# A hybrid mLSTM layer: half of four projections' lo tiles by an adding transfer, and gate_a's modulation on the vector engine

## The chip, the core and the metric

The kernel runs on one core of a Trainium2 chip. A core has five engines that each work through a queue of their own in order: TensorE (PE; its weight loads are listed apart as PEld), VectorE (DVE), ScalarE (ACT), GpSimd (POOL) and SyncE (SP). They meet through semaphores. Transfers between the chip's memory (HBM) and the core's memory (SBUF) run on 16 DMA engines and are issued by SP, ACT or POOL. The metric is the device time of one execution in microseconds. Before the change it is 1696.96 us, the median of three runs (1695.77 to 1698.8).

## What is computed

One layer of a flow-matching backbone on 128 context tokens and 256 latent tokens, model width 2048, all in 32-bit floats.

```python
mod = silu(cond) @ ada_w + ada_b            # six vectors of 2048: shift_a, scale_a, gate_a, shift_f, scale_f, gate_f
h = rmsnorm(x, norm_w[0]) * (1 + scale_a) + shift_a
q, k, v, o, g, u = split(h @ w_in)          # q, k, v, o: 1024 columns each
hm = mlstm_bidir(q, k, v, gates(g))         # 8 heads x 128, chunks of 128 tokens, both directions
hm = rmsnorm(hm) * sigmoid(o)
hp = pool_mixer(u)
mix = concat(hm, hp) @ w_out
x = x + gate_a * rmsnorm(mix, norm_w[1])
h = rmsnorm(x, norm_w[2]) * (1 + scale_f) + shift_f
x = x + gate_f * rmsnorm(square(relu(h @ w1)) @ w2, norm_w[3])
```

The context tokens are modulated by `c_ctx`, the latent tokens by `c`, so each of the six vectors exists twice. Outputs are both token groups and the context's final mLSTM states.

## The kernel before

**Splitting.** TensorE multiplies 32-bit data in a fast format that keeps part of the mantissa (`F32R`). To stay exact, each operand is split into hi, its rounding to that format, and lo = raw - hi, and each product is three matmuls, hi*hi, hi*lo and lo*hi (`mm3`, L142 to L145). A weight tile is 128 x 1024. `load_w` (L122) issues its load on SP (L128, tile `raw`, 3 buffers), makes hi by a copy on ScalarE (L134, 4 buffers) and lo by a subtraction on VectorE (L135, 4 buffers). A raw buffer is free again when lo is done.

**Projections.** `gemm_T` (L168) computes 256 columns of a projection for all 384 tokens. The 2048 rows of the weight come as four tiles (`korder`), so a group of 256 columns has four steps of 24 matmuls. After each step it calls feeds: generators that put one more piece of other work into the program. A `Feed` (L150) has a rate, the mean number of pieces in a step.

**Stages.** First come u, v and the gates' columns (L400 on), then q and k for head pair 0 with the pooling and the gates beside, then q and k for head pairs 1 to 3 with the attention of the pair before beside (L735), then o in four groups (L757), then the output projection `wo` in eight groups, two of them together at the start (L805). Behind it follow the norm, `make_h2` (L915) and the MLP. POOL issues the loads and stores of the attention's states (L579, L685), computes the pow of the norms (L200), and reloads the transposed input for `make_h2` (xTr, L899, 16 transfers of 192 KB).

**Modulation.** A modulation vector is a matrix-vector product with columns of `ada_w`, 8 MB for 1024 columns. It is done in two ways. `ada_mat` (L215) multiplies loaded pieces with the condition on TensorE (L232) and folds the result with L241. `ada_vec` (L261) takes 1024 columns; for each of 16 loads of 512 KB (L269) VectorE multiplies and adds for both conditions (L280, L282), then TensorE sums over partitions (L293), ScalarE copies (L295) and TensorE transposes (L299). Before the change, feed `ada1` runs `ada_mat` for the second half of gate_a (vector 2) at 0.35 pieces a step from q of pair 0 on. Feed `ada2` runs `ada_vec` five times, over scale_f, shift_f and the first half of gate_a, at 1.5 pieces a step in q and k, 1.3 in o, 1.3 in wo. Both must be done when wo ends (L813).

**Order.** Behind the opening projections no order is written out by hand. A scheduler of the recording layer places the instructions of each engine from the program, its dependencies and the buffers.

Of the kernel before, what the change touches and what calls it, by code (L numbers as in the profile page):

```python
# [7 lines left out]
F32 = mybir.dt.float32  # L8
F32R = mybir.dt.float32r
AF = mybir.ActivationFunctionType  # L10
ALU = mybir.AluOpType
# [24 lines left out]
RATE_GS = 0.25  # L36
S_FIRST, S_LAST, N_LAST = 1, 6, 2
LAG = 4
RATES = (1.5, 1.3, 1.3)
RATE_MAT = 0.35  # L40


# [1 line left out]
def hymba_kernel(  # L44
# [6 lines left out]
    nc = tc.nc  # L51
# [13 lines left out]
    def bank(name):  # L65
        return psum.tile([P, 512], F32, tag="ps", name=name)
# [52 lines left out]
    abias = prmT[:, 80:176].rearrange("p (i k) -> p i k", k=KT)  # L119


    def load_w(pieces, name, n=1024, after=(), later=None):  # L122

        raw = wp.tile([P, 1024], F32, tag="raw", name=f"raw_{name}", bufs=3)
        a = pieces[0][1].shape[1]
        rv = raw[:, 0:n].rearrange("p (a b) -> p a b", a=a)
        for off, src in pieces:
            load_w.ins = nc.sync.dma_start(rv[:, :, off:off + src.shape[2]], src).ins  # L128
        hi = wp.tile([P, 1024], F32R, tag="hi", name=f"hi_{name}", bufs=N_W)
        lo = wp.tile([P, 1024], F32R, tag="lo", name=f"lo_{name}", bufs=N_W)  # L130
        with ExitStack() as es:
            for ins in after:
                es.enter_context(tc.issue_after(ins))
            nc.scalar.activation(hi[:, 0:n], raw[:, 0:n], AF.Copy)  # L134
            low = lambda: nc.vector.tensor_tensor(lo[:, 0:n], raw[:, 0:n], hi[:, 0:n].bitcast(F32), op=ALU.subtract)  # L135
            if later is None:
                low()
            else:
                later.append(low)
        return (hi[:, 0:n].rearrange("p (a b) -> p a b", a=a), lo[:, 0:n].rearrange("p (a b) -> p a b", a=a))  # L140

    def mm3(ps, lh, ll, rh, rl, start, stop):  # L142
        nc.tensor.matmul(ps, lh, rh, start=start, stop=False)  # L143
        nc.tensor.matmul(ps, lh, rl, start=False, stop=False)  # L144
        mm3.ins = nc.tensor.matmul(ps, ll, rh, start=False, stop=stop).ins  # L145

    def wview(w):
        return w.rearrange("(k p) n -> p k n", p=P)
# [19 lines left out]
    def gemm_T(w, cols, xs, n, evac, feeds=(), korder=(0, 1, 2, 3), name="g", hold=None):  # L168

        wv = wview(w)  # L170
        acc = {}
        for g, c0 in enumerate(cols):
            for o in range(2):
                acc[g, o] = bank(f"acc_{name}_{c0}_{o}")
        beside = hold or (lambda ki, g: steps_done[-LAG] if len(steps_done) >= LAG else ())
        for ki, kc in enumerate(korder):
            for g, c0 in enumerate(cols):
                hi, lo = load_w([(0, wv[:, 4 * kc:4 * kc + 4, c0:c0 + 256])], f"{name}_{c0}_{kc}", after=beside(ki, g))
                for k in range(4):
                    xh, xl = xs(4 * kc + k)  # L180
                    for o in range(2):
                        mm3(acc[g, o][:, 0:n], hi[:, k, o * P:(o + 1) * P], lo[:, k, o * P:(o + 1) * P],
                            xh[:, 0:n], xl[:, 0:n], ki == 0 and k == 0, ki == 3 and k == 3)
                steps_done.append([])
                for f in feeds:
                    f()
        for g, c0 in enumerate(cols):
            for o in range(2):
                evac(c0 // P + o, acc[g, o])

# [24 lines left out]
    def ada_mat(parts, tags=("ada",), raws=None):  # L215


        n, nk = len(parts), parts[0][2]
        w, nj = nk * P, 8 // nk
        ps = bank(f"ada_{parts[0][0]}_{parts[0][1]}")  # L220
        for b, (i, k0, _) in enumerate(parts):
            c0 = i * D + k0 * P
            for j0 in range(0, 16, nj):
                tag = tags[b % len(tags)]
                raw = raws.pop(0) if raws else None
                if raw is None:
                    raw = (wp if tag == "lo" else adap).tile([P, nj, w], F32, tag=tag, name=f"ada_raw_{i}_{k0}_{j0}", bufs=N_W if tag == "lo" else N_ADA)
                    nc.sync.dma_start(raw, aw[:, j0:j0 + nj, c0:c0 + w])
                for a in range(nj):
                    j = j0 + a  # L230
                    g = j % 4
                    nc.tensor.matmul(ps[32 * g:32 * g + 32, 0:w], cT[:, j, 6 - 2 * b:38 - 2 * b], raw[:, a, :],  # L232
                                     start=b == 0 and j < 4, stop=b == n - 1 and j >= 12)
                if b < n - 1 or j0 + nj < 16:
                    yield
        sb = adap.tile([P, 512], F32, tag="adasb", name=f"ada_sb_{parts[0][0]}_{parts[0][1]}", bufs=1)
        with tc.high_priority():
            nc.scalar.activation(sb[:, 0:w], ps[:, 0:w], AF.Copy)
        yield
        for k in range(nk):  # L240
            nc.tensor.matmul(ps[:, 256 + 8 * k:256 + 8 * k + 2 * n], sb[:, k * P:(k + 1) * P], cst[:, C_SEL, 0:2 * n], start=True, stop=True)  # L241
# [19 lines left out]
    def ada_vec(i, c, n):  # L261


        acc = vec["acc"].tile([P, 2, n], F32, tag="adaacc", name=f"ada_acc_{i}_{c}", bufs=1)
        c0, nj = i * D + c, vec["slab"] // n

        def load(t):
            raw = vec["pool"].tile([P, nj, n], F32, tag="ada", name=f"ada_raw_{i}_{c}_{t}", bufs=vec["bufs"])
            nc.sync.dma_start(raw, aw[:, nj * t:nj * t + nj, c0:c0 + n])  # L269
            return raw  # L270

        raw = load(0)
        yield
        for t in range(16 // nj):
            ahead = load(t + 1) if t < 16 // nj - 1 else None
            for a in range(nj):
                for g in range(2):
                    cj = sg[:, g, nj * t + a:nj * t + a + 1]
                    if t == 0 and a == 0:
                        nc.vector.tensor_scalar(acc[:, g, :], raw[:, a, :], cj, None, op0=ALU.mult)  # L280
                    else:
                        nc.vector.scalar_tensor_tensor(acc[:, g, :], raw[:, a, :], cj, acc[:, g, :], op0=ALU.mult, op1=ALU.add)  # L282
            raw = ahead
            if ahead is not None:
                yield
        yield
        w = n // 2
        nk = w // P
        ps = bank(f"adav_{i}_{c}")
        for h in range(2):  # L290
            for g in range(2):
                r = 32 * (2 * h + g)
                nc.tensor.matmul(ps[r:r + 32, 0:w], ones[:, 0:32], acc[:, g, h * w:(h + 1) * w], start=True, stop=True)  # L293
        sb = vec["pool"].tile([P, 512], F32, tag="adasb", name=f"adav_sb_{i}_{c}", bufs=1)
        nc.scalar.activation(sb[:, 0:w], ps[:, 0:w], AF.Copy)  # L295
        yield
        pf = bank(f"adaf_{i}_{c}")
        for k in range(nk):
            nc.tensor.matmul(pf[:, 4 * k:4 + 4 * k], sb[:, k * P:(k + 1) * P], ident[:, 0:P:32], start=True, stop=True)  # L299
# [100 lines left out]
    for s in range(NS):  # L400
        for ci, (kind, c0, w) in enumerate(chunks):
            k0, nk = ksteps[s]
            hi, lo, n = w_first if s == 0 and ci < 2 else load_chunk(s, ci, h_ins if s == 0 else ())
# [299 lines left out]
        yield  # L703

    def mid_vec():
        for i, q in ((4, 0), (4, 1), (3, 0), (3, 1), (2, 0)):
            yield from ada_vec(i, 1024 * q, 1024)

    ada1 = Feed(ada_mat([(2, 8 + 2 * b, 2) for b in range(4)]), RATE_MAT)
    ada2 = Feed(mid_vec(), RATES[0])  # L710

    def qk(g, feeds):
# [26 lines left out]

    ada2.rate = RATES[1]  # L740
    mixs = [None] * KT
# [296 lines left out]
    pieces = [(a, min(a + NTOK, D)) for a in range(0, D, NTOK)]  # L1038
# [264 lines left out]
```

## Time and profile before

| | |
|---|---|
| median of the runs shown | 1696.96 us |
| profiled execution | 1692.67 us, span 1690.6 us |
| granted TensorE clock, mean | 0.998 |
| HBM read, written | 308.61 MB, 10.51 MB |
| chain that ended last | PE 88%, DVE 6%, DMA 3%, issue 2%, ACT 1% |
| raw_wo: from issue to landing | 4.0 / 5.0 / 7.5 us (least, median, longest) |

Times in views of the profile are microseconds from the start of the span, durations of groups nanoseconds. A row of a stretch gives, for each engine, the busy time and the instructions, then the granted clock, the mean busy share of the 16 DMA engines and what they moved. A row of waits reads: engine, its line and tile, what it waited for; us in total, times, longest. In a row of the timeline stand start, length, engine, line, operation, tiles, and in brackets the idle time before it with what ended it. A row of a tile has the least, median and longest duration in ns. SPq is SP's issuing of transfers.

The chain that ended last lies on TensorE for 88% of the span, so the first question to any change is what it takes from or adds to TensorE's stream, and the second what TensorE would have to wait for.

### The profile page before, as it was taken

Reading aid. Unit: us, or ns where it says so; the run is one execution under the profiler, and the core shown is the slowest. Engines: PE = TensorE matmul, PEld = TensorE weight load, DVE = VectorE, ACT = ScalarE, POOL = GpSimd, SP = SyncE. Lnnn points to the kernel's source line nnn. Section 1 sums busy time; section 2 is a strip of 40 time slices with the busy share of each in tenths; the row PEclk is TensorE's granted clock in tenths of the full one; section 3 lists DMA queues with packets and bytes.
Section 4 is the critical chain, followed back from the end, with each engine's and each line's share of the span. In section 5 each row is a group of like instructions: output and inputs, shape, how many; then the busy total and the mean of one; then the engine's idle time right before and its main releaser. Section 6 shows DMA issues by size and latency. Waiting matters only on the chain.

```text
span 1690.6 us, 28001 instructions
## 1 busy us (share of the span) xinstructions
PE 1663.2 (98%) x11025; PEld 1582.6 (94%) x11025; DVE 1340.0 (79%) x2013; ACT 751.7 (44%) x1225; POOL 133.2 (8%) x181
## 2 busy tenths in 40 slices
PE   6999999999999999999999999999999999999997
PEld 3878899999999989988999999999999999999996
DVE  3677759898989959997798589888588488588688
ACT  4432345555534345543444444444444444444443
POOL 0000002221000024530000000000000000000120
PEclk9999999999999999999999999999999999999999
DMA  9889958777788863754556245444344443433653
GB/s 304 292 287 300 298 164 259 234 250 246 239 285 285 277 224 122 220 155 132 159 173 193 89 137 179 153 150 140 110 150 124 127 137 113 149 122 111 186 184 134
DMA packets 262291, 320.95 MB, mean 190 GB/s; under 512 B 14752, under 2 KB 231440, under 8 KB 261776
## 3 DMA queue, kind: packets, MB, share of 16 engines
q1 hardware_dynamic: 254352, 303.41, 56.3%
q0 software_dynamic: 5856, 13.69, 2.8%
q10 hardware_dynamic: 1952, 2.07, 0.4%
q8 instruction: 86, 1.41, 0.3%
q14 instruction: 45, 0.37, 0.1%
HBM read 308.61 MB, written 10.51 MB: 189 GB/s over the span
## 4 chain that ended last, share of the span: by engine, by line
PE 88%; DVE 6%; DMA 3%; issue 2%; ACT 1%; POOL 0%; DVEq 0%; SPq 0%; ACTq 0%; POOLq 0%
PE acc_w L144 10%; PE acc_w L143 10%; PE acc_w L145 10%; PE y L1137 4%; PE y L1138 4%; PE y L1136 4%; PE u L414 3%; PE v L414 3%; PE acc_wo L143 2%; PE acc_wo L144 2%; PE acc_wo L145 2%; PE ada L232 2%; PE y_yz L1136 2%; PE y_yz L1137 2%; PE y_yz L1138 2%; PE y L980 2%
## 5 line engine op out<-in xcount | busy, mean ns | idle before, releaser
L144 PE MATMUL acc_w<-h2l,hi_w 128*128 128x384 f32 (+1 forms) x1024 | 345.9, 338 | 0.5 <-DVE h2l L930 0.5
L143 PE MATMUL acc_w<-h2h,hi_w 128*128 128x384 f32 (+1 forms) x1024 | 344.4, 338 | 1.2 <-ACT h2h L926 1.2
L145 PE MATMUL acc_w<-h2h,lo_w 128*128 128x384 f32 (+1 forms) x1024 | 345.6, 337 | 0.0
L135 DVE TENSOR_TENSOR lo_w<-raw_w,hi_w 128x1024 fp32r<-128x1024 f32 x152 | 185.4, 1221 | 134.8 <-ACT hi_w L134 134.4
L134 ACT ACTIVATE hi_w<-raw_w 128x1024 fp32r<-128x1024 f32 x152 | 160.7, 1058 | 213.2 <-PE acc_w L144 99.5
L282 DVE SCALAR_TENSOR_TENSOR ada_acc<-ada_raw,sg,ada_acc 128x1024 f32<-128x1024 f32 (+1 forms) x240 | 253.1, 1085 | 2.7 <-DMA ada_raw<-in_ada_w_dram 2.7
L143 PEld LDWEIGHTS acc_w<-h2h,hi_w 128*128 128x128 f32 x1024 | 192.2, 188 | 2.9 <-ACT h2h L926 2.0
L144 PEld LDWEIGHTS acc_w<-h2l,hi_w 128*128 128x128 f32 x1024 | 192.4, 188 | 1.2 <-DVE h2l L930 0.8
L145 PEld LDWEIGHTS acc_w<-h2h,lo_w 128*128 128x128 f32 x1024 | 192.4, 188 | 0.3 <-DVE lo_w L135 0.2
L1122 ACT ACTIVATE hi_t<-w 128x1024 fp32r<-128x1024 f32 x104 | 109.5, 1059 | 116.7 <-DVE w L1158 31.8
L1123 DVE TENSOR_TENSOR lo_t<-w,hi_t 128x1024 fp32r<-128x1024 f32 x104 | 126.3, 1220 | 15.2 <-ACT hi_t L1122 14.9
L1123 DVE TENSOR_TENSOR lo_b<-w,hi_b 128x1024 fp32r<-128x1024 f32 x78 | 95.3, 1221 | 42.2 <-ACT hi_b L1122 41.9
L1122 ACT ACTIVATE hi_b<-w 128x1024 fp32r<-128x1024 f32 x78 | 82.6, 1059 | 101.2 <-PE acc_w L144 67.9
L134 ACT ACTIVATE hi_wo<-raw_wo 128x1024 fp32r<-128x1024 f32 x32 | 34.0, 1064 | 74.9 <-DMA raw_wo<-in_w_out_dram 42.8
L856 ACT ACTIVATE z<-acc_w 128x384 f32<-128x384 f32 x54 | 26.2, 485 | 75.3 <-PE acc_w L145 75.3
L414 PE MATMUL v<-hi_v,hh 128*128 128x384 f32 (+1 forms) x144 | 47.8, 332 | 0.0
L414 PE MATMUL v<-lo_v,hh 128*128 128x384 f32 (+1 forms) x144 | 46.5, 323 | 0.0
L414 PE MATMUL v<-hi_v,hl 128*128 128x384 f32 (+1 forms) x144 | 46.5, 323 | 0.0
L232 PE MATMUL ada<-ada_raw,cT 128*32 128x256 f32 x656 | 45.0, 394 | 1.2 <-DMA ada_raw<-in_ada_w_dram 1.1
L135 DVE TENSOR_TENSOR lo_wo<-raw_wo,hi_wo 128x1024 fp32r<-128x1024 f32 x32 | 38.9, 1221 | 7.3 <-ACT hi_wo L134 7.2
L143 PE MATMUL acc_k<-hh,hi_k 128*128 128x384 f32 x128 | 44.5, 348 | 0.0
L143 PE MATMUL acc_o<-hh,hi_o 128*128 128x384 f32 x128 | 44.1, 344 | 0.0
(2250 smaller groups left out, 4517.1 us busy)
## 6 DMA issues: line engine op xcount, KB each, us to landing
ada_raw<-in_ada_w_dram SPq DMA_DIRECT2D x170, 512.0 KB, 4.8
raw_w<-in_w_dram SPq DMA_DIRECT2D x152, 512.0 KB, 4.2
w<-in_w_dram SPq DMA_DIRECT2D x104, 512.0 KB, 4.2
raw_wo<-in_w_out_dram SPq DMA_DIRECT2D x32, 512.0 KB, 5.0
raw_u<-in_w_in_dram SPq DMA_DIRECT2D x16, 512.0 KB, 8.6
raw_q<-in_w_in_dram SPq DMA_DIRECT2D x16, 512.0 KB, 5.0
raw_k<-in_w_in_dram SPq DMA_DIRECT2D x16, 512.0 KB, 5.0
raw_o<-in_w_in_dram SPq DMA_DIRECT2D x16, 512.0 KB, 4.9
```

Of the source, the lines that this page charges most:

```text
L134: nc.scalar.activation(hi[:, 0:n], raw[:, 0:n], AF.Copy)
L135: low = lambda: nc.vector.tensor_tensor(lo[:, 0:n], raw[:, 0:n], hi[:, 0:n].bitcast(F32), op=ALU.subtract)
L143: nc.tensor.matmul(ps, lh, rh, start=start, stop=False)
L144: nc.tensor.matmul(ps, lh, rl, start=False, stop=False)
L145: mm3.ins = nc.tensor.matmul(ps, ll, rh, start=False, stop=stop).ins
L282: nc.vector.scalar_tensor_tensor(acc[:, g, :], raw[:, a, :], cj, acc[:, g, :], op0=ALU.mult, op1=ALU.add)
L414: nc.tensor.matmul(acc[i][:, 0:n], h[k0 + k][a][:, i * P:(i + 1) * P], (hi, lo)[b][:, k, :], start=k == 0 and a + b == 0, stop=k == nk - 1 ...
L1122: nc.scalar.activation(hi, raw, AF.Copy)
L1123: nc.vector.tensor_tensor(lo, raw, hi.bitcast(F32), op=ALU.subtract)
L1136: nc.tensor.matmul(acc, xh, wh, start=start and j == 0, stop=False)
L1137: nc.tensor.matmul(acc, xh, wl, start=False, stop=False)
L1138: nc.tensor.matmul(acc, xl, wh, start=False, stop=stop and j == 3)
```

## The change

In the second and fourth step of each group of q, k, o and wo, `load_w` is called with `by_dma`. ScalarE then writes -hi into the lo tile, and POOL issues a transfer that adds raw to it in place. That is 40 of the 80 tiles. The second half of gate_a moves from `ada_mat` to a sixth `ada_vec`, with the rates raised so that six fit, and `ada_vec` has one more `yield`, between ScalarE's copy and the transposing matmuls, so that a step of other work lies between them.

```diff
-RATES = (1.5, 1.3, 1.3)
+LO_BY_DMA = ('q', 'k', 'o', 'wo')
+RATES = (1.85, 1.7, 1.55)
@@ load_w
+            if by_dma:
+
+                nc.scalar.activation(lo[:, 0:n], hi[:, 0:n].bitcast(F32), AF.Copy, scale=-1.0)
+                nc.gpsimd.dma_start(lo[:, 0:n].bitcast(F32), raw[:, 0:n], accum_op=ALU.add)
+            elif later is None:
-            if later is None:
                 low()
@@ gemm_T
+                by_dma = name in LO_BY_DMA and ki % 2 == 1
+                hi, lo = load_w([(0, wv[:, 4 * kc:4 * kc + 4, c0:c0 + 256])], f"{name}_{c0}_{kc}", after=beside(ki, g), by_dma=by_dma)
@@ ada_vec
         nc.scalar.activation(sb[:, 0:w], ps[:, 0:w], AF.Copy)
+        yield
         yield
@@ hymba_kernel
-        for i, q in ((4, 0), (4, 1), (3, 0), (3, 1), (2, 0)):
-            yield from ada_vec(i, 1024 * q, 1024)
-
-    ada1 = Feed(ada_mat([(2, 8 + 2 * b, 2) for b in range(4)]), RATE_MAT)
+        for i in (4, 3, 2):
+            for q in range(2):
+                yield from ada_vec(i, 1024 * q, 1024)
+
+    ada1 = Feed(iter(()), RATE_MAT)
```

Lines behind the first hunk are one higher in the changed kernel, behind `load_w` five, behind `gemm_T`'s hunk six, behind the yield seven and behind `mid_vec` eight.

The rows below are the built programs' orders. In tile names the buffer's number stands last; the number before it in a weight tile is the tile's place among the four of its group (wo takes them in the order 2, 3, 0, 1, so 3 and 1 are the adding ones).

ScalarE in wo, before, one group's copies to hi and, between them, the squares and copies of the group before:

```order
L134 ACTIVATE hi_wo_1_5698<-raw_wo_1_5696 128x1024
L134 ACTIVATE hi_wo_2_5745<-raw_wo_2_5743 128x1024
L295 ACTIVATE adav_sb_1024_5657<-adav_1024_5652 128x512
L134 ACTIVATE hi_wo_3_5779<-raw_wo_3_5777 128x1024
L134 ACTIVATE hi_wo_0_5817<-raw_wo_0_5815 128x1024
```

and in the changed program:

```order
L135 ACTIVATE hi_wo_1_5675<-raw_wo_1_5673 128x1024
L139 ACTIVATE lo_wo_1_5676<-hi_wo_1_5675 128x1024
L135 ACTIVATE hi_wo_2_5728<-raw_wo_2_5726 128x1024
L135 ACTIVATE hi_wo_3_5760<-raw_wo_3_5758 128x1024
L139 ACTIVATE lo_wo_3_5761<-hi_wo_3_5760 128x1024
L135 ACTIVATE hi_wo_0_5798<-raw_wo_0_5796 128x1024
```

Each adding tile has a second copy, -hi into lo, directly behind its first.

POOL at the end of wo, before: nothing of wo's weights, and the reloads of xT follow the store of the final normaliser:

```order
L685 DMA out_dram<-C_3_0_1_4413 128x2x128
L200 TENSOR_TENSOR rsh<-rsh,mhalf 128x2 x3
L765 DMA out_dram<-n_o 16x128
L899 DMA xTr_6348<-xT_dram 128x384
L899 DMA xTr_6350<-xT_dram 128x384
```

and in the changed program, where the reloads come behind the last adding transfer:

```order
L140 DMA lo_wo_1_6159<-raw_wo_1_6156 128x1024
L140 DMA lo_wo_3_6244<-raw_wo_3_6241 128x1024
L140 DMA lo_wo_1_6314<-raw_wo_1_6311 128x1024
L907 DMA xTr_6360<-xT_dram 128x384
L907 DMA xTr_6362<-xT_dram 128x384
```

Sixteen adding transfers of wo stand in POOL's queue, and the xTr loads now follow all of them.

SP in wo, before, loads of the weight (`raw_wo`) and of `ada_w` for the vector matvec (`ada_raw`, last but one number: the load's place among 16):

```order
L128 DMA raw_wo_2_5897<-in_w_out_dram 128x4x256
L269 DMA ada_raw_0_6_5927<-in_ada_w_dram 128x1024
L128 DMA raw_wo_3_5935<-in_w_out_dram 128x4x256
L269 DMA ada_raw_0_7_5931<-in_ada_w_dram 128x1024
L128 DMA raw_wo_0_5969<-in_w_out_dram 128x4x256
L269 DMA ada_raw_0_8_5965<-in_ada_w_dram 128x1024
L128 DMA raw_wo_1_6003<-in_w_out_dram 128x4x256
```

and in the changed program:

```order
L129 DMA raw_wo_1_5998<-in_w_out_dram 128x4x256
L275 DMA ada_raw_1024_4_5956<-in_ada_w_dram 128x1024
L275 DMA ada_raw_1024_5_5990<-in_ada_w_dram 128x1024
L129 DMA raw_wo_2_6045<-in_w_out_dram 128x4x256
L275 DMA ada_raw_1024_6_5994<-in_ada_w_dram 128x1024
L275 DMA ada_raw_1024_7_6029<-in_ada_w_dram 128x1024
L129 DMA raw_wo_3_6083<-in_w_out_dram 128x4x256
```

Between the first load of wo's weight and the first of w1's, SP has 40 loads for the vector matvec now where it had 34, beside the same 32 of the weight and 8 for gate_f. In q and k of pairs 1 to 3 there are 32 loads of `ada_w` where there were 35, and in o 21 where there were 24.

More of the change, by code (lines that the diff above doesn't have):

```diff
@@ L119, in hymba_kernel, with load_w @@
     abias = prmT[:, 80:176].rearrange("p (i k) -> p i k", k=KT)
-    def load_w(pieces, name, n=1024, after=(), later=None):
+    def load_w(pieces, name, n=1024, after=(), later=None, by_dma=False):
         raw = wp.tile([P, 1024], F32, tag="raw", name=f"raw_{name}", bufs=3)
@@ L177, in gemm_T @@
             for g, c0 in enumerate(cols):
-                hi, lo = load_w([(0, wv[:, 4 * kc:4 * kc + 4, c0:c0 + 256])], f"{name}_{c0}_{kc}", after=beside(ki, g))
+                by_dma = name in LO_BY_DMA and ki % 2 == 1
+                hi, lo = load_w([(0, wv[:, 4 * kc:4 * kc + 4, c0:c0 + 256])], f"{name}_{c0}_{kc}", after=beside(ki, g), by_dma=by_dma)
                 for k in range(4):
```

## The prediction

> **What bounds the kernel now.** I read the page's busy shares first, then stretches of the run with the DMA share beside the engines, then who waits for whom in the stage that is fullest.
>
> ```profile
> PE 1663.2 (98%) x11025; PEld 1582.6 (94%) x11025; DVE 1340.0 (79%) x2013; ACT 751.7 (44%) x1225; POOL 133.2 (8%) x181
> ```
>
> TensorE is busy 98% of the span, so a change can only win by taking work off it, and can lose wherever it makes it wait. The stretches below are the opening projections (0 to 190), two short samples, q and k of head pairs 1 to 3 (257 to 394), o (394 to 478) and the output projection wo (478 to 618).
>
> ```profile
> core 0: us, PE busy (x) PEld busy (x) DVE busy (x) ACT busy (x) POOL busy (x), PEclk, DMA share, GB/s
> 0.00:190.00 190.00, 174.18 (x1248) 136.52 (x1249) 118.81 (x260) 69.13 (x117) 4.73 (x15) 0.99 0.90 298
> 10.00:15.00 5.00, 0.95 (x2) 0.36 (x2) 0.00 (x0) 3.93 (x9) 0.00 (x0) 1.00 1.02 395
> 257.00:394.00 137.00, 137.00 (x904) 130.17 (x903) 125.77 (x215) 72.11 (x204) 29.95 (x26) 1.00 0.76 245
> 394.00:478.00 84.00, 84.00 (x534) 79.28 (x538) 73.44 (x110) 40.74 (x95) 9.23 (x8) 1.00 0.75 247
> 478.00:618.00 140.00, 140.00 (x819) 137.05 (x812) 124.54 (x141) 50.31 (x76) 9.49 (x17) 1.00 0.88 289
> 500.00:510.00 10.00, 10.00 (x59) 10.00 (x58) 10.00 (x9) 3.09 (x3) 0.00 (x0) 1.00 1.00 343
> ```
>
> In all stages that change, TensorE has no idle time. Second come two things at once in wo: VectorE with 124.54 of 140 us, and the 16 DMA engines with a share of 0.88. In 500 to 510 they stand at 1.00 and move 343 GB/s; the fastest stretch of the trace moves 395. In the opening, where transfers set the pace, the share is 0.90 over 190 us, so 0.88 is already near what a long stage reaches.
>
> ```profile
> SPq L269 <- DVE ada_acc L282: 56.3, 27, 3.6
> SPq L128 <- DVE lo_wo L135: 27.3, 28, 2.4
> PEld acc_wo L143 <- ACT hi_w L134: 0.8, 1, 0.8
> ```
>
> These are waits in wo. Loads wait for VectorE to free their buffers (56.3 + 27.3 us), while TensorE's own waits are tenths of a us: the buffers' depth hides VectorE. So work taken from VectorE buys nothing by itself here.
>
> **The change, part by part.** *gate_a's second half leaves TensorE.* The matrix form ran 16 steps (four column pieces by four loads) of eight L232 matmuls, spread over q, k and o, and one L241 step.
>
> ```profile
> 295.34 0.34 PE L145 MATMUL acc_k<-hh,lo_k 128*128 128x384 f32 x1
> 295.61 0.64 PE L232 MATMUL ada<-ada_raw,cT 128*32 128x256 f32 x8
> 296.18 0.44 PE L143 MATMUL acc_k<-hh,hi_k 128*128 128x384 f32 x1
> ...
> 482.82 0.33 PE L145 MATMUL acc_wo<-mx11h,lo_wo 128*128 128x384 f32 x1
> 482.99 0.51 PE L241 MATMUL ada<-cst,ada_sb 128*128 128x8 f32 x4
> 483.35 0.42 PE L143 MATMUL acc_wo<-mx12h,hi_wo 128*128 128x384 f32 x1
> ...
> 538.65 0.34 PE L145 MATMUL acc_wo<-mx15h,lo_wo 128*128 128x384 f32 x1
> 538.92 1.06 PE L293 MATMUL adav<-ada_acc,cst 128*32 128x512 f32 x8
> 539.91 0.44 PE L143 MATMUL acc_wo<-mx0h,hi_wo 128*128 128x384 f32 x1
> ...
> 543.85 0.34 PE L144 MATMUL acc_wo<-mx3l,hi_wo 128*128 128x384 f32 x1
> 544.02 0.34 PE L145 MATMUL acc_wo<-mx3h,lo_wo 128*128 128x384 f32 x1
> 544.20 0.95 PE L299 MATMUL adaf<-cst,adav_sb 128*128 128x4 f32 x8
> 545.01 0.42 PE L143 MATMUL acc_wo<-mx4h,hi_wo 128*128 128x384 f32 x1
> ```
>
> Matmuls of the stream follow each other every 0.175 us (543.85 to 544.02). From 295.34 to 296.18 are 0.84, so an L232 step costs 0.66, and 16 of them 10.6 us. L241 costs 483.35 - 482.82 - 0.175 = 0.36. The sixth vector matvec that replaces them costs one L293 step, 539.91 - 538.65 - 0.175 = 1.09, and one L299 step, 545.01 - 544.02 - 0.175 = 0.82. TensorE's net is -10.6 - 0.36 + 1.09 + 0.82 = **-9.1 us**. Of it the 10.6 lie in q, k and o; wo gains 1.9 - 0.36 of work, so its 140 us become 141.5.
>
> *VectorE and ScalarE.*
>
> ```profile
> L282 DVE SCALAR_TENSOR_TENSOR ada_acc<-ada_raw,sg,ada_acc 128x1024 f32<-128x1024 f32 (+1 forms) x240 | 253.1, 1085 | 2.7 <-DMA ada_raw<-in_ada_w_dram 2.7
> 558.84 4.87 DVE L282 SCALAR_TENSOR_TENSOR ada_acc<-ada_raw,sg,ada_acc 128x1024 f32<-128x1024 f32 x4
> L135 DVE TENSOR_TENSOR lo_wo<-raw_wo,hi_wo x32: 1214/1221/1226, 471.1 to 602.5; 128x1024 fp32r<-128x1024 f32 x32
> L134 ACT ACTIVATE hi_wo<-raw_wo x32: 1048/1062/1084, 464.2 to 601.4; 128x1024 fp32r<-128x1024 f32 x32
> ```
>
> 40 of the 80 lo parts of q, k, o and wo leave VectorE: 40 x 1.22 = 48.8 us off. 32 matvec instructions come in; the wide ones take 4.87 / 4 = 1.22 (the group's mean of 1.085 mixes in narrower ones): 39 us on. VectorE ends about 10 us lighter and about as full per stage, because the new rates spread the sixth matvec in proportion. I cost this at nothing: the buffers hid VectorE before. If that cover fails, a VectorE that is later by one lo part costs 1.2 us once. ScalarE gets 40 copies more, 40 x 1.06 = 42 us; in wo that is 50.31 + 17 of 140 us, hidden.
>
> *The adding transfers.* The trace has none, so I bound one. It moves 0.524 MB, reading raw and lo and writing lo. From below: nothing, if it runs only where the engines are idle; then one copy at the trace's fastest rate, 0.524 / 395 = 1.33 us of all 16 engines. From above: two full loads at wo's mean rate, 289 / 0.88 = 328 GB/s at full share, so 2 x 1.60 = 3.2. I take two passes at the fastest rate, **2.65 us**, since it has twice a copy's input and reads no HBM.
>
> The Trainium skill, "Collectives: The Full Stack", section "The bandwidth ceiling: the fold count and why AG ≠ RS ≠ AR", says the same of sums made in the DMA datapath: the add is free, but two source reads halve the rate of a copy (62.28 against 32.35 GB/s measured). By it the sum is the one below, by a single pass the first rival's; no run here shows it yet.
>
> *wo's transfers, added up.* Before: 289 GB/s x 140 us = 40.5 MB, which at 343 GB/s take 118 us. The vector matvec issues 40 loads there instead of 34: 6 x 0.524 / 343 = 9.2 us. The adding transfers: 16 x 2.65 = 42.4. Together 169.6. The 16 reloads of xT (192 KB each, 3.1 MB, 9.2 us) are used only behind wo and can slip. That leaves 160.4 us of transfers for a stage with 141.5 us of TensorE work: **+18.9 us**, shown as weight tiles that land late, first at ScalarE's hi copy, then at TensorE. The same sum for q and k: 245 x 137 / 343 = 97.9, less three loads (4.6), plus 12 x 2.65 = 31.8, is 125 us beside the 137 less nine L232 steps, 131; for o 60.5 - 4.6 + 21.2 = 77 beside 84 less five, 80.7. Both fit, barely; I count nothing there and keep it for the upper end.
>
> *The first adding tile* has the shortest lead.
>
> ```profile
> 201.59 1.06 ACT L134 ACTIVATE hi_q<-raw_q 128x1024 fp32r<-128x1024 f32 x1 [2.41 <-DMA raw_q<-in_w_in_dram]
> ...
> 208.96 0.34 PE L145 MATMUL acc_q<-hh,lo_q 128*128 128x384 f32 x1
> ...
> x1t<-x_dram POOLq DMA_DIRECT2D x15, 192.0 KB, 4.1
> raw_wo<-in_w_out_dram SPq DMA_DIRECT2D x32, 512.0 KB, 5.0
> ```
>
> A 192 KB transfer of POOL lands 4.1 us after its issue; 2 x 0.524 MB instead of 0.197 at 395 GB/s add 2.2, so 6.3. Hi ends at 202.65, the negated copy at 203.7, the sum lands at 210.0, and TensorE wants it at 208.96: **+1.0**. I count no later tile.
>
> **Sum:** -9.1 + 18.9 + 1.0 = +10.8 us on the profiled execution's 1692.67 (span 1690.6). The runs' median is 1696.96, 4.3 higher, and the change is carried over to it: **1708 us**.
>
> **The rivals.** *It fits (ends on the other side).* If one adding transfer costs a single pass, 1.33 us, wo's transfers are 118 + 9.2 + 21.3 - 9.2 = 139.3 beside 141.5: TensorE stays the bound and -9.1 remains, 1688. It decides at 16 transfers x p = 23.5, so p = 1.5 us: below it the gain is whole. For it speak TensorE's short waits and that these transfers don't load HBM; against it the share of 0.88, which was measured with 74 loads in wo and no adding transfer.
>
> ```profile
> q1 hardware_dynamic: 254352, 303.41, 56.3%
> q0 software_dynamic: 5856, 13.69, 2.8%
> ```
>
> The page counts SP's queue (q1) and POOL's (q0) as shares of the same 16 engines, so a transfer from POOL is not free of SP's. The Trainium skill, "DMA: Bandwidth & Descriptors", section "Issuing engines are not separate DMA queues", states it as a rule, against this change; the trace has too little on q0 to test it.
>
> *Both cancel.* With p near 2.1 us the overflow is about 9 us, and the time stays within 3 us of 1697.
>
> *The raw ring.* Three raw buffers serve alternately a VectorE tile and an adding tile. The first holds its buffer 5.0 + 1.06 + 1.22 = 7.3 us at least, the second 5.0 + 1.06 + 1.06 + T, with T from POOL's issue to landing. Two turns of the ring are six steps of 24 x 0.175 = 4.2 us, 25.2. So T and all in-order waits may take 25.2 - 14.4 = 10.8; with T = 6.3 there are 4.5 to spare. At T = 13 wo loses 2.2 / 6 x 32 = 12 us: 1700. TensorE's four lo buffers give nearly the same point. This is latency and not load: it would show with the DMA share well below 1.
>
> **How the numbers follow.** DMA engines overfull in wo 0.44 (1708); raw ring 0.12 (1700); it fits 0.32 (1688); both cancel 0.12 (1697). Faster or slower counts from 0.2%, 3.4 us, which is about what a measurement can tell. So faster 0.32, same 0.12, slower 0.56. The range goes from 1687 (the whole of -9.1 and a little of VectorE's relief) to 1724: at 3.2 us each, with no slip and the share's own 0.88 x 140 = 123 us, the overflow would be 42 us and the time about 1730, of which I leave the end out.
>
> **What would show it.** Right: in the changed profile the stretch of wo is some 19 us longer, its DMA share is 0.95 or more, ScalarE's hi_wo waits for raw_wo and not for TensorE, and TensorE's waits name hi or lo of wo; up to the end of o the kernel is 9 to 11 us ahead. Wrong, on the fast side: wo stays at 141 us with a share near 0.95 and q0's share shows 1.3 us for each transfer. Wrong, by the ring: the share stays below 0.9 and SP waits for adding transfers to free raw. Wrong at the root: the loss stands in q, k and o, where POOL's queue, with the pow of the head norm and the loads of C in it, makes VectorE wait for POOL.

## The result, and the profile after

The changed kernel takes 1760.15 us (median of five runs, 1756.28 to 1764.25) beside 1695.90 for the kernel before (1693.68 to 1698.80): a ratio of **1.0376**, 95% interval 1.0361 to 1.039. It is slower, as forecast, but by 64 us instead of 11, outside the range.

The busy shares of the changed kernel's page answer to the first line of the prediction:

```profile
PE 1676.9 (95%) x10909; PEld 1597.4 (91%) x10909; DVE 1335.7 (76%) x2001; ACT 788.1 (45%) x1265; POOL 166.5 (9%) x221
```

TensorE has 116 instructions fewer and is yet busy 14 us longer, in a span 66 us longer. Where that is shows in the time from a stage's first matmul to that of the next (read from the timelines; the last column runs from wo's end to the span's end):

| us | q, k of pair 0 | q, k of pairs 1 to 3 | o | wo | behind |
|---|---|---|---|---|---|
| before | 52.5 | 138.3 | 84.8 | 139.5 | 1072.4 |
| after | 53.0 | 152.0 | 91.1 | 177.8 | 1079.6 |
| difference | +0.5 | +13.7 | +6.3 | **+38.3** | +7.2 |
| forecast | -0.3 | -5.9 | -3.3 | +20.4 | 0 |

The stretches of the changed kernel, with the columns as in the prediction's:

```profile
256.00:408.00 152.00, 138.29 (x856) 134.60 (x854) 123.72 (x215) 82.35 (x216) 38.83 (x38) 0.98 0.87 255
408.00:500.00 92.00, 85.34 (x497) 81.67 (x497) 79.38 (x114) 45.89 (x101) 15.88 (x15) 0.96 0.85 251
500.00:677.00 177.00, 150.94 (x805) 144.48 (x804) 119.39 (x125) 65.64 (x91) 22.71 (x33) 0.92 0.97 290
```

In wo the DMA engines now stand at 0.97 (0.88 before), and TensorE idles for 26 of 177 us. Second, its granted clock is 0.92: TensorE is busy for 150.9 us with work that took 140. In q, k and o it idles too, though the share there is only 0.87 and 0.85. TensorE's waits from 200 to 700 us say for what:

```profile
PE acc_wo L150 <- DMA lo_wo<-raw_wo: 21.8, 8, 5.9
PE hT L707 <- DVE hs L671: 9.0, 2, 5.4
PE acc_o L150 <- DMA lo_o<-raw_o: 4.9, 3, 3.8
PE inter L658 <- DVE C L641: 4.7, 3, 2.8
PE acc_wo L150 <- DVE lo_wo L136: 4.2, 1, 4.2
PE adaf L306 <- ACT adav_sb L301: 3.6, 1, 3.6
PE acc_q L150 <- DMA lo_q<-raw_q: 2.6, 2, 1.8
```

In wo and o it waits for the sums, in q and k mostly for the attention (hs is the normed head output, C the state). Upstream in wo, ScalarE's hi waits for loads (33.9 us before the change), and SP, which issues them in order, waits for the adding transfers to free the raw buffers; the two rows are ScalarE's and SP's, from 500 to 678 us:

```profile
ACT hi_wo L135 <- DMA raw_wo<-in_w_out_dram: 83.0, 24, 11.1
...
SPq L129 <- DMA lo_wo<-raw_wo: 79.4, 15, 9.5
```

Three explanations were set against each other. **LOAD**: the 16 engines have too much to move. **RING**: a raw buffer is held until the sum lands, so loads start late; latency, not load. **VECTOR**: the moved matvec delays VectorE's part of the attention by itself.

### The profile page after: what moved, and what is told of

It is laid out like the page before. It is cut to its first block, busy times and chain, and to the rows that moved or that the text cites. A ratio compares the mean times of both kernels' runs of the same rounds, so it can differ in the third digit from the quotient of the medians.

```text
span 1757.0 us, 27895 instructions
## 1 busy us (share of the span) xinstructions
PE 1676.9 (95%) x10909; PEld 1597.4 (91%) x10909; DVE 1335.7 (76%) x2001; ACT 788.1 (45%) x1265; POOL 166.5 (9%) x221
## 4 chain that ended last, share of the span: by engine, by line
PE 72%; DMA 13%; DVE 6%; issue 5%; ACT 2%; POOL 1%; SPq 0%; DVEq 0%; POOLq 0%; ACTq 0%
PE acc_w L148 9%; PE acc_w L149 9%; PE acc_w L150 9%; PE y L1145 4%; PE y L1144 4%; PE y L1146 4%; PE u L421 4%; PE v L421 4%; DMA lo_wo<-raw_wo 3%; DMA raw_wo<-in_w_out_dram 2%; PE y_yz L1144 2%; PE y_yz L1145 2%; PE y_yz L1146 2%; PE ada L238 2%; DMA ada_raw<-in_ada_w_dram 2%
## 5 line engine op out<-in xcount | busy, mean ns | idle before, releaser
L288 DVE SCALAR_TENSOR_TENSOR ada_acc<-ada_raw,sg,ada_acc 128x1024 f32<-128x1024 f32 (+1 forms) x270 | 289.7, 1108 | 15.2 <-DMA ada_raw<-in_ada_w_dram 15.1
L135 ACT ACTIVATE hi_wo<-raw_wo 128x1024 fp32r<-128x1024 f32 x32 | 33.9, 1061 | 94.5 <-DMA raw_wo<-in_w_out_dram 88.6
L150 PE MATMUL acc_o<-hh,lo_o 128*128 128x384 f32 x128 | 44.7, 349 | 4.9 <-DMA lo_o<-raw_o 4.9
L150 PE MATMUL acc_q<-hh,lo_q 128*128 128x384 f32 x128 | 43.8, 342 | 2.6 <-DMA lo_q<-raw_q 2.6
```

## The experiments

Ratios are to the kernel before as it ran beside each, with 95% intervals; most times are good to 3 or 4 us, a difference of two to 4 or 5. The stages are those of the table above, from one profile each. What each kernel is stands below the table. no_sum, eighth, load_paced, slot52 and the three with ring4 in their name have 52 slot tiles (general buffers, `N_SLOT`), the others the change's 55.

| kernel | us | ratio | q, k 1-3 | o | wo | behind |
|---|---|---|---|---|---|---|
| no_sum | 1696.0 | 1.0008 (0.9993-1.0024) | 134.6 | 79.9 | 141.9 | 1078.7 |
| no_sum55 | 1688.6 | 0.9961 (0.9945-0.9976) | 136.8 | 79.7 | 143.4 | 1074.0 |
| eighth | 1712.1 | 1.0092 (1.0068-1.0115) | 137.9 | 80.5 | 156.3 | 1080.3 |
| eighth55 | 1705.2 | 1.0062 (1.004-1.0084) | 142.8 | 81.0 | 150.1 | 1074.7 |
| copy | 1728.1 | 1.0184 (1.0163-1.0205) | 148.4 | 81.6 | 164.2 | 1080.4 |
| after | 1760.2 | 1.0376 (1.0361-1.039) | 152.0 | 91.1 | 177.8 | 1079.6 |
| load_paced | 1744.7 | 1.0285 (1.026-1.0309) | 152.1 | 81.6 | 171.1 | 1086.2 |
| slot52 | 1764.3 | 1.0409 (1.0388-1.0429) | 142.3 | 88.1 | 180.7 | 1086.3 |
| ring4 | 1747.5 | 1.0301 (1.0285-1.0316) | 151.7 | 84.3 | 168.1 | 1086.0 |
| eighth_ring4 | 1711.1 | 1.0085 (1.0052-1.0118) | 144.4 | 81.0 | 148.6 | 1084.8 |
| every4 | 1737.6 | 1.0236 (1.0211-1.0262) | 144.7 | 79.5 | 179.2 | 1076.1 |
| every4_ring4 | 1726.6 | 1.017 (1.0129-1.0212) | 144.2 | 83.8 | 165.3 | 1080.3 |
| add_only | 1739.8 | 1.0263 (1.0242-1.0284) | 159.0 | 85.5 | 160.0 | 1074.8 |
| gate_only | 1726.0 | 1.0171 (1.0154-1.0188) | 147.2 | 92.1 | 155.9 | 1077.7 |
| ht_late | 1763.3 | 1.0392 (1.0376-1.0408) | 154.2 | 90.7 | 178.4 | 1082.6 |
| pool_lo | 1742.4 | 1.0271 (1.0253-1.029) | 151.3 | 97.6 | 167.2 | 1074.4 |
| o_only | 1735.6 | 1.023 (1.0212-1.0249) | 146.5 | 99.8 | 156.6 | 1075.7 |

**The price of a transfer, by how much it moves.** The first try, with 52 slot tiles:

```diff
-nc.gpsimd.dma_start(lo[:, 0:n].bitcast(F32), raw[:, 0:n], accum_op=ALU.add)
+nc.gpsimd.dma_start(lo[:, 0:128].bitcast(F32), raw[:, 0:128], accum_op=ALU.add)
```

> The changed kernel, but each adding transfer sums only the first 128 of the 1024 columns (the other columns of lo stay -hi, so seven eighths of the sum are left out), and the pool of slots has 52 tiles, not 55. ScalarE's negated copy, POOL's issue, and VectorE's relief are unchanged. Theory LOAD (the adding transfers' 2.9 us of all 16 DMA engines each overfill wo): 16 x 0.36 = 6 us instead of 46 in wo, so wo is back from 178 to 142-146 us, q and k to 3 pairs in 131-140, the whole 1690-1712 us. Theory RING (a raw buffer is held from the load's landing until the sum lands, latency and not load): the fixed part of the landing, some 5 of 8.3 us, stays, so wo keeps about half of its loss, 155-165 us, the whole 1720-1740. Theory VECTOR (the sixth matvec's new rates put up to five wide matvec instructions of 1.28 us into the attention chain, hs comes late, and TensorE waits for it at hT): q and k of pairs 1 to 3 keep 148-153 us and their hT waits of 9 us, whatever the transfers cost; alone it leaves the whole near 1712.

It took 1712.1 us, 52 less than its control `slot52` (below), with wo at 156.3: LOAD expected at most 146, RING 155 to 165. The whole lies at LOAD's upper end (1712), below RING's 1720, and VECTOR's 148 to 153 us in q and k did not come. `no_sum` deletes the transfer's line.

> The changed kernel without the adding transfers: lo of an adding tile stays -hi (the sum of these 40 tiles is left out), ScalarE's copies and the matvec of gate_a on VectorE as in the change; 52 slot tiles. All theories that put the loss on the adding transfers: TensorE's saving of 9.1 us is left, 1685-1692, q and k of pairs 1 to 3 in 130-134 us, wo in 140-143. VECTOR (the matvec's new rates delay the attention chain by themselves): q and k of pairs 1 to 3 stay at 136 or more with waits at hT, the whole 1694-1705.

It took 1695.95 us, wo 141.9. But with 52 slot tiles the matvec began at 195 us instead of 251, so that VectorE had 96 us of work in q and k instead of 123, and wo was followed by 5 to 7 us more (1078.7 for no_sum55's 1074.0, 1086.3 in slot52 for 1079.6). Why was not taken apart; the likely reason is that the matvec's buffers then lie in memory that is free earlier. The pair was run again with 55.

> As no_sum (the sum of the 40 adding tiles is left out, no adding transfer), with the change's own 55 slot tiles: 52 had moved part of the matvec ahead and cost 4 to 7 us behind wo. This prices the rest of the change by itself: matvec moved to VectorE, ScalarE's 40 copies, VectorE's relief. If TensorE's saving of 9.1 us is all there is: 1686-1689. If the moved matvec also delays the attention chain or the seam behind wo: 1690-1697.

> As the eighth (seven eighths of each sum are left out), with 55 slot tiles, so that it can be set beside the changed kernel and the paced load, which both start the matvec only behind the first q and k. What stands between no_sum55 and this is the price of having to wait for a small transfer (its landing of 3 to 5 us, and raw held until then); what stands between this and the change is the price of the other seven eighths. By the earlier runs: 1704-1712, q and k of pairs 1 to 3 in 140-147 us, wo 150-157.

`copy` takes out only `accum_op`.

> The change with plain copies of raw into lo in place of the adding transfers (the subtraction of hi is left out in these 40 tiles), everything else the same. If an adding transfer's time on the 16 engines comes from its second read, a copy costs about half, 1.3-1.6 us each by the share of POOL's queue (2.9 for the sum), and the loss falls by a third to a half: 1722-1742, wo 157-168. If moving within SBUF is slow by itself, the copy costs 2.5-3 us and the whole stays at 1750-1765.

POOL's queue (q0; packets, MB, share of the 16 engines' span), first in no_sum55:

```profile
q0 software_dynamic: 5856, 13.69, 2.8%
```

In eighth55:

```profile
q0 software_dynamic: 11616, 16.31, 4.0%
```

In copy:

```profile
q0 software_dynamic: 11616, 34.66, 5.9%
```

And in the changed kernel:

```profile
q0 software_dynamic: 11616, 34.66, 9.3%
```

Copy and sum have the same packets and bytes, and the sum takes more time. For 40 transfers, less the 2.8% of a span of 1690: 0.040 x 1701 - 47.3 = 20.7, 0.059 x 1727 - 47.3 = 54.6, 0.093 x 1757 - 47.3 = 116.1 us. So an eighth takes 0.52 us of all engines, a copy **1.36** and an adding transfer **2.90**. And the ladder prices the change: everything but the sums **-6.7** us (no_sum55), having to wait for a small transfer **+16.6** (eighth55), one whole pass of data in its place **+22.9** (copy), the sum in the copy's place **+32.0** (with the second read; POOL's issue takes 0.85 us instead of 0.53, too). Without transfers TensorE's stream is nearly whole. The rows are wo in no_sum55 and, at the same share of the DMA engines, wo in copy:

```profile
473.00:616.00 143.00, 141.00 (x807) 137.42 (x807) 120.45 (x127) 65.53 (x91) 9.12 (x17) 0.99 0.91 306
482.00:646.00 164.00, 145.39 (x809) 139.16 (x808) 121.08 (x127) 64.76 (x90) 17.52 (x33) 0.97 0.91 312
```

**Load that nobody waits for.** Behind each eighth came a full adding transfer of a scratch tile onto itself.

```diff
+nc.gpsimd.dma_start(scr, scr, accum_op=ALU.add)
```

> As the eighth, with one adding transfer more behind each eighth: a 128x1024 scratch tile onto itself, which nobody reads and which holds no raw and no lo buffer. So the load of the full sum is back, without anyone waiting for it. LOAD: wo as in the changed kernel, 170-180 us at a DMA share of 0.97, the whole 1740-1765. RING: as the eighth alone within 5 us. VECTOR: q and k as in the eighth.

This tested nothing of wo. With nothing to wait for, all 40 were placed ahead of the first adding tile on POOL, and TensorE stood still for 55.8 us (1812 us in all); wo, at 155.5, had no more load than the eighth's. It gave a price alone: 12 of them between 240 and 306 us, one every 4.8 us, with POOL's queue at 51% of the engines' time, so 0.51 x 66 / 12 = 2.8 us each. The next run ties each to its eighth in POOL's order.

> As the eighth (only 128 of 1024 columns are summed by each adding transfer, seven eighths of the sum are left out), with a full 128x1024 adding transfer of a scratch tile onto itself behind each eighth, this time ordered behind it in POOL's queue, so that all 40 are spread as the adding tiles are; nobody reads the scratch tile, and it holds no raw and no lo buffer. In the run before this one they had all run ahead of the first adding tile, at 2.8 us of the 16 engines each, and loaded nothing behind it; there wo took 155.5 us, the eighth's 156.3. LOAD (the 16 engines overfull): wo 172-180 us with a DMA share of 0.96 or more, the whole 1745-1770. RING (raw held until the sum lands): wo 154-162, the whole 1708-1725. Both at work: wo 163-171.

```profile
485.00:656.00 171.00, 150.68 (x809) 144.49 (x809) 121.75 (x127) 66.51 (x93) 33.26 (x43) 0.94 1.03 308
```

wo is at 171.1 us with the engines full (the share adds up the packets' times, so it can pass 1), nearly the changed kernel's, and the whole 39.5 us above eighth55, though nobody waits for the added data. Some of that is not load: 11.5 us of it lie behind wo, where kernels with 52 slot tiles are longer. From q of pair 1 to the end of wo load_paced is 31 us above eighth55, the changed kernel 47. The awaited eighths hardly land later for it (6.1 us after their issue in wo, for 5.7 in eighth55), but the loads of wo's weight do (7.5 us for 5.6, medians). So LOAD is the larger part of what lies between the eighth and the full sum, at most some two thirds: an eighth and its partner take 3.3 us of the engines together, more than a full sum. The rest, 16 us or more, is what having to wait for the full sum adds.

**The ring.** `slot52` is the control with 52 slot tiles, `ring4` has a fourth raw buffer besides.

```diff
+load_w.n += 1
+if load_w.n % 4 == 3 and vec.get("own"):
+    raw = vec["own"].tile([P, 1024], F32, tag="rawx", name=f"raw_{name}", bufs=1)
+else:
     raw = wp.tile([P, 1024], F32, tag="raw", name=f"raw_{name}", bufs=3)
```

> The changed kernel with 52 slot tiles, not 55: the control of the others. All theories: 1760 within 0.4%, wo 175-180 us.

> The changed kernel with 52 slot tiles and, from pair 1 of q and k to the end of wo, a fourth raw buffer (every fourth tile of the ring takes it). RING: SP no longer waits for adding transfers to free raw (79 us in wo), loads start about one step (4.2 us) earlier, and wo loses at least 20 of its 36 us over TensorE's 141.5: the whole 1725-1742. LOAD: the 16 engines stay full, wo stays at 172-178 us, the whole within 6 us of the control; the loads only wait longer from issue to landing (6.5 us now, 8 or more then). VECTOR: q and k unchanged within 3 us.

```profile
493.00:661.00 168.00, 150.40 (x809) 143.46 (x807) 119.38 (x125) 65.71 (x92) 22.78 (x33) 0.94 0.99 307
```

The buffer gives 17 us back against the control, 13 of them in wo. Against the change itself, whose matvec starts as late as ring4's (slot52's starts early), it gives 13 in all and 17 up to the end of wo. In wo that is less than RING's 20 and more than LOAD's 6, so both work. The row shows how they combine: loads that start earlier fill the engines to 0.99 and 307 GB/s, and there it ends. The same buffer on the eighth:

> The eighth with the fourth raw buffer. RING: the eighth's remaining loss in wo, 156.3 - 141.5 = 15 us, is SP's wait for the adding transfers (78 us there) and goes: wo 141-146, the whole 1692-1700. If the remaining loss is the chain from the load's landing over two ScalarE copies and the sum to TensorE, with buffers of no influence: wo 153-157 and the whole 1708-1714.

It gains nothing beyond the spread (1711.1 beside the eighth's 1712.1). Its wo of 148.6 lies between the two forecasts and below the eighth's 156.3; but eighth55, whose matvec starts as late as here (the eighth's starts early), has 150.1 without the buffer, and 142.8 in q and k beside 144.4. So with small transfers the buffers are not what costs 16.6 us.

`every4` sums only the fourth step's tile (`ki == 3`).

> The change with an adding transfer for every fourth tile (20 in place of 40; VectorE computes the other 20). From no_sum55 (1688.6) 40 adding transfers cost 71 us, 1.8 each. If the cost is in proportion: 36 us, and VectorE's 24 us of work come back, for which about 13 are free: 1725-1735. If a threshold of the DMA share decides (0.91 without them in wo, full at 0.97), the first 20 are cheaper: 1700-1715.

Half the transfers give back a third of the loss, and wo none at all:

```profile
480.00:659.00 179.00, 156.19 (x853) 147.83 (x852) 142.53 (x147) 61.91 (x89) 13.97 (x21) 0.97 0.89 277
```

LOAD alone can't give 179 us at 0.89. VectorE has 142.5 us of work again, and SP waits both for its buffers and for the sums. One raw buffer more tells the two apart:

> The kernel with every fourth tile summed by an adding transfer, with the fourth raw buffer (52 slot tiles, as in ring4). Its wo took 179.2 us at a DMA share of only 0.89, with VectorE busy 141.5 us. RING: SP's in-order loads stand behind the adding transfers (43 us of SP's waits in wo) and VectorE's buffers, so one buffer more brings wo to 155-165 and the whole to 1712-1726. VECTOR (141.5 us of VectorE's work plus its own waits sets wo's length): wo stays at 173-180, the whole within 6 us of 1737.6. LOAD can't explain 179 us at this share, so it predicts no change either.

wo falls to 165.3 and the whole to 1726.6, both at the upper ends of RING's forecasts. So there the ring costs 14 us of wo, and VectorE's work isn't what sets the length.

**The two halves of the change apart.** `add_only` keeps the adding transfers and gives the second half of gate_a and the rates back to the kernel before; `gate_only` has `LO_BY_DMA = ()`.

> The adding transfers alone: all of gate_a's second half back on TensorE, the rates of before, VectorE 39 us emptier than in the change, 6 loads fewer in wo. LOAD: wo's transfers fall by 6 x 1.6 = 9 us against the change, so wo takes 165-170 us, the whole 1740-1755 with TensorE's 9 us back. RING: wo stays at 175-182 us, the whole 1760-1775. VECTOR: q and k of pairs 1 to 3 fall from 152 us to 139-142 though TensorE has 8 us more to do.

> gate_a's move to VectorE with the new rates, and no adding tile: all lo parts on VectorE. VectorE had 125.8 + 73.4 + 124.5 = 324 us of work from pair 1 to the end of wo; with 39 us more, 363 us beside 352 of TensorE's. If that decides, the kernel loses those 11 us instead of TensorE's 9, and some for the attention chain: 1700-1712, q and k of pairs 1 to 3 in 142-150 us. If buffers and the ends of the stages absorb it, 1688-1692, and the adding transfers were needless.

Both halves lose alone. add_only loses 44 us; its wo is 18 us shorter than the change's, 8 more than the six loads that it lacks explain at 1.6 us each (where the 8 come from was not taken apart). q and k are longer by 7 us, of which the nine L232 steps that are back on TensorE make 6; VECTOR had them fall to 139 to 142, so it falls there. gate_only loses 30: VectorE, with all lo parts and the sixth matvec, is late at TensorE throughout; for a cover that fails, the prediction had 1.2 us once. TensorE's waits in gate_only:

```profile
PE acc_wo L150 <- DVE lo_wo L136: 10.7, 4, 5.5
PE acc_o L150 <- DVE lo_o L136: 8.2, 4, 3.0
PE acc_q L150 <- DVE lo_q L136: 6.6, 4, 2.7
```

**Is the wait at hT a loss of its own?** `ht_late` has one more `yield` ahead of the head transposes.

> The change with the head transposes hT one step later in TensorE's order, so that the attention chain has 4.2 us more. If the waits at hT (9.0 us and two stretches at half clock) are a loss of their own: q and k of pairs 1 to 3 fall from 152 to 140-145 us, the whole to 1748-1753. If late loads and sums only show there first and the next consumer waits in its place: q and k 149-153, the whole 1756-1764.

The 9.0 us at hT are gone and nothing is won: TensorE's waits in q and k of pairs 1 to 3 are 13.3 us in all, where they were 13.7. The three longest now:

```profile
PE acc_q L150 <- DMA lo_q<-raw_q: 4.5, 2, 3.5
PE adaf L306 <- ACT adav_sb L301: 3.6, 1, 3.6
PE inter L658 <- DVE C L641: 3.1, 2, 2.2
```

So hT was where lateness showed, not where it arose. ScalarE works in order, and hi of a weight tile stands among the attention's activations. In the changed kernel's q and k, hi_k waits 22.4 us for its loads; in no_sum55 hi_k waits there for TensorE alone, and all of ScalarE's waits for loads are tenths of a us, and hT waits 3.1 us instead of 9.0. This link is read from the waits; no run moved hi in ScalarE's order.

**Two tries at a version that beats both.** `pool_lo` lets GpSimd subtract, `o_only` has `LO_BY_DMA = ('o',)`.

```diff
-nc.scalar.activation(lo[:, 0:n], hi[:, 0:n].bitcast(F32), AF.Copy, scale=-1.0)
-nc.gpsimd.dma_start(lo[:, 0:n].bitcast(F32), raw[:, 0:n], accum_op=ALU.add)
+nc.gpsimd.tensor_tensor(lo[:, 0:n], raw[:, 0:n], hi[:, 0:n].bitcast(F32), op=ALU.subtract)
```

> The change with the 40 lo parts computed by GpSimd (one subtraction each from raw and hi, as VectorE does it) instead of ScalarE's negated copy and the adding transfer. No transfer is added. GpSimd's 128x384 addition takes 1.4 us in this trace, so one of 128x1024 at most 3.8, 60 us of wo's 141. If the transfers were the whole loss and GpSimd runs beside VectorE undisturbed: 1686-1692, better than both kernels. If the two engines slow each other by a third or more in wo (VectorE has 119 us there): 1700-1725, with VectorE's STT above 1.4 us.

> The change with adding transfers in o alone, the stage with the lowest DMA share (0.76 without them) : 8 transfers x 2.9 = 23 us of the 16 engines beside 0.24 x 80 = 19 free. The eighth and the paced load showed o hardly longer (81.0 and 81.6 us for 79.7), so the 8 should cost 2 to 6 us by their landing, and VectorE is 10 us emptier than with gate_a's move alone. If it hides: 1688-1695, the candidate for a version that beats the kernel before. If VectorE, too full in q, k and wo, decides: 1695-1706.

Neither does. GpSimd's subtraction takes 2.4 us in q and 3.9 in wo:

```profile
L139 POOL TENSOR_TENSOR lo_wo<-raw_wo,hi_wo 128x1024 fp32r<-128x1024 f32 x16 | 61.7, 3861 | 90.5 <-ACT hi_wo L135 90.5
```

Its rows show late lo parts and a late attention; which of the two engines' slowing costs what was not taken apart. In o_only, o is 8 us longer than in gate_only, which has no transfer: even in o, whose share is below that of wo and of q and k before the change and after it, eight sums cost more than VectorE's relief brings. No kernel here that computes the whole is faster than the one before. An adding transfer that reads the weights from HBM, and so frees raw early, was not tried.

## Why the prediction was wrong

The kernel is slower, as forecast, but only in part for the reasons given. Of the signs named for being right, wo's share of 0.95 or more, hi's wait for raw_wo and TensorE's for lo of wo came; "up to the end of o the kernel is 9 to 11 us ahead" did not, since wo began 21 us late.

**TensorE's net of -9.1 us: right.** no_sum55 is 6.6 us faster than the kernel before by its ratio (4 to 9 by the interval's ends), with 5.1 us of waits at hT and for VectorE's lo_wo in TensorE's stream that the kernel before hasn't. TensorE's busy time there is 1655.3, 7.9 less than before, with 6.8 us at half clock in it.

**VectorE and ScalarE at nothing: right with the relief, mis-sized without.** With all 48.8 us taken off, no_sum55 shows little of it. Without, in gate_only, the cover is gone at a price of 37 us over no_sum55, not 1.2 once.

**2.65 us for an adding transfer: right in kind and near in size.** It took 2.90, and a copy 1.36, just above the lower bound of one pass. The Trainium skill, "Collectives: The Full Stack", section "The bandwidth ceiling: the fold count and why AG ≠ RS ≠ AR", has a sum with two reads at half a copy's rate; the runs agree, with 2.1. The first rival (it fits, below 1.5 us) falls with the price, and its rule falls too: a copy is below 1.5 us, and still copy takes 1728 us where the rival had 1688. Its wo needs 118 + 9.2 + 16 x 1.36 = 149 us of the engines by the prediction's terms, 139.8 without the reloads of xT, beside 141.5 of TensorE's; 0.91 x 164 = 149 is what it shows, but in 164 us. The Trainium skill's rule in "DMA: Bandwidth & Descriptors", section "Issuing engines are not separate DMA queues", is borne out by load_paced: POOL's transfers slow SP's loads (of wo, 7.5 us for eighth55's 5.6) though no one waits for them.

**wo: the transfers' sum was right, what followed from it wasn't.** The queues in the changed kernel's stretch of 500 to 677 us (packets, MB, share of 16 engines):

```profile
q1 hardware_dynamic: 26274, 40.31, 66.4%
q0 software_dynamic: 3153, 10.94, 30.1%
```

That is 117.5 + 53.3 = 170.8 us of all engines; the prediction had 169.6. It then took off 9.2, since the reloads of xT "are used only behind wo and can slip", and set the rest against engines that are never idle. The prediction also had 0.88 for near what a long stage reaches. But the reloads were issued at 661 to 675 us, within wo, as in the kernel before, and the engines reached 0.97: 170.8 / 0.97 = 176. So the excess over 141.5 was 36 where the prediction had 18.9. The 0.97 is measured and not explained by this sum, and wo in copy takes 164 us with the engines at 0.91, no more than in no_sum55, where it takes 143. ring4 shows the other reading of the same number: with earlier loads the engines reach 0.99, and wo is 168.

**q, k and o: "both fit, barely; I count nothing there". This is the step that failed.** They were to gain 9 us from pair 1 on and lost 20, more than half of the miss. The sums themselves were near: 125 and 77 us of transfers, where the shares give 0.87 x 152 = 132 and 0.85 x 91 = 77. What failed is the rule that transfers which fit beside TensorE's work cost nothing. With three raw buffers and loads in order, a mean share of 0.87 does not mean that each load comes in time. eighth55, whose transfers add little load, already has q and k at 142.8, 6 us above no_sum55:

```profile
253.00:395.00 142.00, 134.94 (x852) 131.95 (x851) 121.55 (x214) 82.43 (x215) 40.58 (x38) 0.99 0.75 231
```

The share is 0.75, and a fourth raw buffer leaves it at 144.4, so the landing remains: even an eighth lands 4.0 (k) or 4.4 us (q, medians) after its issue, behind two copies on ScalarE. With the full load the sums land after 5.7 and 7.4, and it is 152. Nor does the mean share alone decide: o takes 81.6 us at 0.93 in load_paced, where TensorE is busy for 79.8 of 81, and 91.1 at 0.85 in the changed kernel. The named sign of this ("the loss stands in q, k, o") came, but not by VectorE waiting for POOL's pow: that wait is 4.5 us in all, 5.4 before.

**The first adding tile, +1.0: near.** Of acc_q's two waits for lo_q the one in pair 0 is 1.8 us.

**What the sum lacked: each long wait is paid twice.** Stretches around one wait in wo, and the matmuls ahead of it and behind:

```profile
586.00:590.00 4.00, 3.71 (x22) 3.38 (x20) 3.49 (x8) 2.61 (x6) 0.85 (x1) 1.00 0.97 310
590.00:594.00 4.00, 0.00 (x0) 0.00 (x0) 0.20 (x1) 2.11 (x2) 0.85 (x1) 0.99 1.04 263
594.00:600.00 6.00, 4.42 (x14) 4.42 (x15) 1.23 (x1) 1.06 (x1) 0.00 (x0) 0.50 1.06 326
601.00:607.00 6.00, 6.00 (x38) 4.91 (x37) 3.89 (x5) 2.73 (x3) 0.80 (x1) 1.00 0.98 333
```

```profile
589.20 0.34 PE L148 MATMUL acc_wo<-mx12h,hi_wo 128*128 128x384 f32 x1
589.37 0.34 PE L149 MATMUL acc_wo<-mx12l,hi_wo 128*128 128x384 f32 x1
595.58 0.69 PE L150 MATMUL acc_wo<-mx12h,lo_wo 128*128 128x384 f32 x1 [5.88 <-DMA lo_wo<-raw_wo]
596.07 0.52 PE L148 MATMUL acc_wo<-mx12h,hi_wo 128*128 128x384 f32 x1
596.39 0.52 PE L149 MATMUL acc_wo<-mx12l,hi_wo 128*128 128x384 f32 x1
```

After 5.9 us of waiting the granted clock (third column from the right) is 0.50, and matmuls follow each other every 0.32 us instead of 0.175. The changed kernel has nine such stretches of 3.4 or 6.8 us between 300 and 690 us, the kernel before none. Five of them, 27 us, lie in wo. There TensorE is busy for 150.9 us against 141.0 in no_sum55, for two instructions fewer: 10 us, beside 24 more of idling. The Trainium skill, "TensorE: Matmul & The Clock Gate", section "HAM oscillation — how this bites in real kernels", gives the rule (no TensorE gap above about 3.4 us, or it goes on at half rate); the prediction should have put it on each tile that it forecast late. The traces here are stricter: half clock followed more than half of the waits of 2 to 3 us too (counts below).

**The seam behind wo, +7.2:** 3.6 us are the wait at adaf, where the sixth matvec's last transposes come just behind wo's end, followed by 6.8 us at half clock. In no_sum55 the whole stretch behind wo is only 1.6 us longer than before. The rest was not taken apart.

**The raw ring**, a rival at 0.12 with 1700, is a part of the loss rather than another case: 13 to 17 us under full load, nothing measurable with the eighth's. Its arithmetic (T up to 10.8 us) took T = 6.3 and a landed load in 5.0; in wo the medians are 8.3 and 6.5. Put in, the loads leave 25.2 - 17.4 = 7.8 us for T: by its own arithmetic the ring binds, by a little.

## What to carry to other kernels

- Work that a vector engine hands to transfers is paid on the 16 DMA engines that bring the weights; here each us of them cost 0.5 to 0.7 us of the kernel (22.9 us for 0.84 x 40, 32.0 for 1.54 x 40). Add it to the stage's sum before, count nothing as slipping that is issued in the stage, and expect that a stage can lose time well below a share of 1 where loads are issued in order into three buffers.
- A wait forecast on a stream that never waited is not its own length alone: above 2 to 3 us, add what the half clock costs behind it.
- Price both halves of a coupled change. Here the gain was 7 us (no_sum55, 9 of TensorE's work by the prediction), and the relief that made room for it cost 72.

## What the runs showed of the hardware

- In the 19 profiles, between 200 and 720 us, 58 of 59 waits of TensorE above 3 us had a stretch at half clock within them or beginning at most 3.5 us behind them (the one without is of 3.3 us, in eighth_load), 36 of 60 between 2 and 3 us, and 7 of 68 between 1 and 2.
- An adding transfer of 512 KB within SBUF takes 2.90 us of the 16 engines, a copy 1.36 (one pass at 385 GB/s); POOL's issue takes 0.85 us; a sum lands 5.1 / 8.3 / 10.0 us (least, median, longest) after its issue in wo, and 4.5 with little else in flight (the scratch tile's, eighth_load from 240 to 306 us).
- GpSimd's subtraction of 128 x 1024 took 2.4 us in q and 3.9 in wo.
